# Smaller token lists for the large experts: 11 and 7 blocks in place of 12 and 8, with mixed blocks of four equal tiles

## The chip, the cores and the metric

The kernel runs on one core of a Trainium2 chip. The metric is the time of one execution in device microseconds (us); the time before is the median of three runs. Bytes are counted in thousands and millions here; a "piece" of weights is 1.05 MB.

## What is computed

Two layers of a diffusion backbone over 256 latent and 256 context tokens of width 1024. Layer 0 mixes by grouped attention and a Fourier branch, layer 1 by differential attention; after each stands a mixture of 16 experts, of which every token takes two:

```
tok = h.reshape(-1, shape[-1])
g_idx = argmax(tok @ w_group + b_group)
e_sel = (tok @ w_router + b_router) of that group
top_p, top_i = lax.top_k(softmax(e_sel), 2)
for each expert:  y = (silu(tok @ wg) * (tok @ wu)) @ wd
                  acc += gate[:, None] * y
```

Each expert's three matrices are 1024 by 512, 1024 by 512 and 512 by 1024, in float32. Layer 0 sends 512 tokens through the mixture, layer 1 only the 256 latent ones.

## The kernel before, in words

**Lists and blocks.** The kernel does not run all tokens through all experts. It sorts the experts of a layer by their token counts (rank 0 has most; two experts in layer 0 and four in layer 1 are left out of the sorting and stand at the last ranks) and gives rank r a list of `CAPS[layer][r]` places (line 32). `PLAN` (line 37) packs the lists into blocks of 128 places, which `block_plan` (line 55) turns into lists of tiles (first place, width, rank): `("m", r)` is one list of 128, `("p", r, s)` two tiles of 64, `("q", ...)` four tiles of 32, and `("w", 0, 1)` cuts the two lists of 192 into two whole blocks and one block of two tiles of 64. That makes 12 blocks in layer 0 and 8 in layer 1. Tokens beyond a list's places go to a slow overflow pass at the layer's end, which runs only if a list overflows (line 1752).

**Products.** A block b has three products: G (gate), U (up) and D (down), 8 chunks of 512 columns each, 24 in all. In layer 0 `products` (line 73) orders them G U of block b, then D of block b-1; in layer 1 the order is written out in `TURNS` (line 69). `gate_up` and `down` (lines 1645 and 1673) issue them. A block of one list in layer 0 is `solo`: the weights are split into a high and a low part by ScalarE and VectorE (line 317, 318) and each chunk is three matmuls with full rows (lines 321 to 323). Every other block multiplies float32 directly (lines 1658 and 1691): each tile of the block is one matmul per chunk into its own stripe of output partitions, and the trace has two rows for each such matmul.

**Lists in layer 0.** `fetch_rows` (line 1265) makes the row numbers of a block: for each of 4 groups of tokens and both choices of expert VectorE compares places with numbers (`hot`, line 1399, output `oh`), and TensorE multiplies (line 1275, output `tok`); then the rows are gathered by an indirect DMA. D writes its result to the scratch tensor `yd` by DMAs on ScalarE's queue (line 1709), two for each tile. In layer 1 rows are picked by matmuls (line 1326, `pick`) and spread back by matmuls (line 1596, `sp`).

**Weights.** Each of an expert's three matrices is two pieces `we`. A piece is loaded once into a room; there are 16 rooms in layer 0 and 18 in layer 1, and a load waits until the room's last piece has been read. The loads stand in one queue on SP (line 216) in the order in which the products first use them (`Experts`, line 993). For ranks that are sorted SP must first read the rank's expert from `perm` (line 1020), which the routing makes. The loads of SP and the writes of `yd` use the same eight completion semaphores in turn, so that a load whose turn falls on the semaphore of a write waits for that write to land. Which instruction stands where on TensorE, VectorE and ScalarE is set by a scheduler when the kernel is built.

Of the kernel before, what the change touches and what calls it, by code (L numbers as in the profile page):

```python
# [11 lines left out]
F32 = mybir.dt.float32  # L12
F32R = mybir.dt.float32r
BF16 = mybir.dt.bfloat16
I32 = mybir.dt.int32
AF = mybir.ActivationFunctionType
ALU = mybir.AluOpType
AX = mybir.AxisListType

P = 128  # L20
# [9 lines left out]


CAPS = (
    (192, 192) + (128,) * 4 + (64,) * 10,
    (192, 192) + (128,) * 2 + (32,) * 12,
)

PLAN = (
    (("p", 14, 15), ("m", 2), ("p", 12, 13), ("m", 3), ("p", 10, 11), ("w", 0, 1), ("m", 4), ("m", 5), ("p", 8, 9),
     ("p", 6, 7)),
    (("q", 12, 13, 14, 15), ("m", 3), ("m", 2), ("w", 0, 1), ("q", 8, 9, 10, 11), ("q", 4, 5, 6, 7)),  # L40
)
MAXSLOTS = max(sum(c) for c in CAPS)

# [1 line left out]
def bases(layer):  # L45

    out, n = [0] * NE, 0
    for _, *rs in PLAN[layer]:
        for r in rs:
            out[r] = n  # L50
            n += CAPS[layer][r]
    return out


def block_plan(layer):

    base, blocks = bases(layer), []
    for kind, *rs in PLAN[layer]:
        if kind == "w":
            pair = [(base[r] + 128, 64, r) for r in rs]  # L60
            ones = [[(base[r], 128, r)] for r in rs]
            blocks += [pair] + ones if layer else [ones[0], pair, ones[1]]
        else:
            blocks.append([(base[r], 128 // len(rs), r) for r in rs])
    return blocks

TURNS = ("G0 U0 G1 U1 D0 D1 G6 G4 U6 U4 G3 G5 D6 U3 D4 U5 D3 D5 G7 G2 U2 U7 D2 D7")


def products(layer):
# [3 lines left out]
    if layer:  # L76
        return [("GUD".index(t[0]), int(t[1:])) for t in TURNS.split()]
    out, n = [], len(block_plan(layer))
# [87 lines left out]
def hybrid_kernel(ctx: ExitStack, tc: tile.TileContext, A: dict, dbg=None):  # L166
    nc = tc.nc
    V, S, T, G = nc.vector, nc.scalar, nc.tensor, nc.gpsimd
# [25 lines left out]
    def right(name):  # L194
        return Open(name, "right")
# [26 lines left out]
    def mm(name="mm"):  # L222
        return psum.tile([P, 512], F32, name=name, tag="mm", bufs=5)
# [4 lines left out]
    def aux(name):  # L228
        return psum.tile([P, 512], F32, name=name, tag="aux", bufs=1)
# [25 lines left out]
    def C(name):  # L255
        a, b = CC.at[name]
        return cst[:, a:b]
# [16 lines left out]
    ones = pool.tile([P, P], BF16, name="ones")  # L274
    V.memset(ones, 1.0)
    tokid = pool.tile([P, 4, 2], BF16, name="tokid")
# [766 lines left out]
    def moe(l, ntb, experts, yp, yT, finish, w_o, place, after_loads):  # L1043
# [151 lines left out]
        def tl(shape, name, dt=F32):  # L1195
            return rt.tile([P] + shape, dt, name=name)
# [63 lines left out]
        blocks = block_plan(l)  # L1260
# [3 lines left out]
        un = right("units")  # L1264
# [3 lines left out]
        def fetch_rows(i, hot):  # L1268

            ps = aux("tok")  # L1270
            for tb in range(ntb):
                for k in range(2):
                    o = un.tile([P, P], BF16, name="oh", bufs=2)
                    hot(o, tb, k)
                    T.matmul(ps[:, 0:2], o, tokid[:, tb, :], start=(tb == 0 and k == 0),
                             stop=(tb == ntb - 1 and k == 1))
            ix = un.tile([P, 1], I32, name="ix", bufs=8)
            with nc.allow_low_precision("whole numbers below 512"):
                V.reduce_sum(ix, ps[:, 0:2], axis=AX.X)
            xg[i] = un.tile([P, D], F32, name="xg", bufs=2)  # L1280
            G.indirect_dma_start(out=xg[i], out_offset=None, in_=h2d[0:NT, :],
                                 in_offset=bass.IndirectOffsetOnAxis(ap=ix[:, 0:1], axis=0))
# [92 lines left out]
        slot, gate, ridx = [], [], []  # L1375
# [3 lines left out]
        slots = tl([2, ntb], "slots")  # L1379
        V.reduce_sum(slots, tmp, axis=AX.X)  # L1380
        slot = [slots[:, i, :] for i in range(2)]


        def runs(i):

            out = []
            for s0, n_, _ in blocks[i]:
                if out and sum(out[-1]) == s0:
                    out[-1] = out[-1][0], out[-1][1] + n_
                else:  # L1390
                    out.append((s0, n_))
            return out

        def fetch(i):

            def hot(o, tb, k):
                c = 0
                for s0, n_ in runs(i):
                    V.tensor_scalar(o[:, c:c + n_], C("iota128")[:, 0:n_], float(s0), slot[k][:, tb:tb + 1],
                                    op0=ALU.add, op1=ALU.is_equal)  # L1400
                    c += n_

            fetch_rows(i, hot)
# [50 lines left out]
        hots, rel = {}, {}  # L1454
# [85 lines left out]
        def combine(tb):  # L1540

            ya = got.pop(tb)
            S.activation(ya[0], ya[0], AF.Copy, scale=early[0][:, tb, :])
            V.scalar_tensor_tensor(ya[1], ya[1], early[1][:, tb, :], ya[0], op0=ALU.mult, op1=ALU.add)
            V.tensor_tensor(out=ya[1], in0=ya[1], in1=g2[:, tb // 2, :], op=ALU.mult)
            V.tensor_tensor(out=xt[:, tb, :], in0=xt[:, tb, :], in1=ya[1], op=ALU.add)
# [65 lines left out]
        def a_turn(bi, q):  # L1612
            if q == 0:
                aTs[bi] = [un.tile([P, 4, P], F32R if solo[bi] else F32, name="aT", bufs=AB)
                           for _ in range(1 + solo[bi])]
            pt = tr()
            for f in range(2):
                c = 256 * q + 128 * f
                T.transpose(pt[:, 128 * f:128 * f + 128], sgs[bi][:, c:c + 128], ident)
            a = [t[:, 2 * q:2 * q + 2, :] for t in aTs[bi]]  # L1620
            src = pt[:, 0:256].rearrange("p (k t) -> p k t", k=2)
            if solo[bi]:
                split(*a, src)
            else:
                V.tensor_copy(a[0], src)
            if q:
                sgs.pop(bi)
# [11 lines left out]
        def split_to(i, k):  # L1639
            for c in chunks[len(parts):]:  # L1640
                if c[0] > i + 1 or KT * (c[0] - i) + c[1] > k + WB - 1:
                    break
                parts[c] = [un.tile([P, 512], F32R, name=name, bufs=WB) for name in ("wh", "wl")]
                split(*parts[c], weights_at(*c))
# [27 lines left out]
        def down(bi, amid, final):  # L1672
            late = bi not in aTs
            if late:
                a_turn(bi, 0)
            if final:
                a_turn(bi, 1)
                combine(2)
            ps = [mm("dn") for h in range(2)]
            for f in range(4):  # L1680
                if f == 1 and late and not final:
                    a_turn(bi, 1)
                amid(f)
                for h in range(2):
                    split_to(now[0], 2 * f + h)
                    if solo[bi]:
                        mm3(ps[h], [t[:, f, :] for t in aTs[bi]], parts[now[0], 2 * f + h], f == 0, f == 3)
                        continue
                    c = 0
                    for _, n_, r in blocks[bi]:  # L1690
                        T.matmul(ps[h][c:c + n_], aTs[bi][0][:, f, c:c + n_],  # L1691
                                 part(experts.w[r, 2], f)[:, 512 * h:512 * h + 512], start=(f == 0), stop=(f == 3))
                        c += n_
            spread_some(4)
            if l:
                if bi == [b for which, b in ops if which == 0][-1]:

                    S.activation(lam[:, 6:7], aTs[bi][0][:, 0, 0:1], AF.Sqrt, bias=eps, scale=0.0)
                ship(bi, ps)
            elif final:  # L1700
                finish_ctx(ps)
            else:
                c = 0
                y = [un.tile([P, 512], F32, name="y", bufs=1 if l else YB) for h in range(2)]
                V.tensor_copy(y[0], ps[0])
                S.copy(y[1], ps[1])
                for s0, n_, _ in blocks[bi]:
                    for h in range(2):
                        sent = S.dma_start(yd[s0:s0 + n_, 512 * h:512 * h + 512], y[h][c:c + n_, :])
                    c += n_  # L1710
                if bi == len(blocks) - 2:
                    for _ in range(6):
                        experts.issue(1, queue=S)
# [38 lines left out]
        with tc.If(rv > 0):  # L1752
# [16 lines left out]
            with tc.For_i(0, NE, 1) as e:  # L1769
# [3 lines left out]
                with tc.If(nc.values_load(some[0:1, 0:1], min_val=0, max_val=1) > 0):  # L1773
                    ws = []
                    for i in range(3):
                        ws.append([])
                        for h in range(2):
                            w, src = weights(pick, i, h)
# [4 lines left out]
                    for tb in range(ntb):  # L1783
# [4 lines left out]
                        for half in range(2):  # L1788
                            pt = tr()
                            for j in range(4):  # L1790
                                kt = 4 * half + j
                                c = slice(128 * kt, 128 * kt + 128)
                                if l == 0:
                                    T.transpose(pt[:, 128 * j:128 * j + 128], xr[:, c], ident)
                                for n in range(len(exact)):
                                    T.matmul(pt[:, 128 * j:128 * j + 128], exact[n][tb][:, c], identb, start=(n == 0),
                                             stop=(n == len(exact) - 1))
                            S.copy(xT_[:, 4 * half:4 * half + 4, :], pt.rearrange("p (k t) -> p k t", k=4))
                        gu = []
                        for which in range(2):  # L1800
                            ps = tr("gu")
# [11 lines left out]
                        for h in range(2):  # L1813
                            ps = tr("dn")
                            for f in range(4):
# [3 lines left out]
                                                   op0=ALU.mult, op1=ALU.mult)  # L1819
# [7 lines left out]
        if l:  # L1827
            for tb, h in itertools.product(tbs, range(2)):
                c = slice(512 * h, 512 * h + 512)
# [132 lines left out]
```

## Time and profile before

| | |
|---|---|
| median of 3 runs (lowest to highest) | 1064.69 us (1059.69 to 1064.75) |
| the profiled execution | 1066.53 us, of it 1064.7 us span |
| TensorE (PE) busy | 985.5 us, 93% |
| VectorE (DVE) busy | 556.2 us, 52% |
| ScalarE (ACT) busy | 397.3 us, 37% |
| bytes moved by DMA | 309.85 MB, 291 GB/s on average |
| mean granted TensorE clock | 0.976 |

The span is the time from the first to the last instruction; 1.8 us of the execution lie outside it. Busy time of TensorE overlaps waits in part, since ends of matmuls are modelled, so lengths of stretches are read from starts of instructions in the timeline. Products of layer 0's experts run from 274 to 568 us of the span, those of layer 1's from 825 to 1050 us.

### The profile page before, as it was taken

What the parts mean: (1) busy time and instruction counts of PE and PEld (TensorE: products, weight loads), DVE (VectorE), ACT (ScalarE), POOL (GpSimd) and SP (SyncE); (2) the same over time, 40 slices, a digit from 0 to 9 for tenths busy, and PEclk for the clock granted to TensorE, in tenths of its full rate; (3) what the DMA queues carried; (4) which work ended last, traced back from release to release, by engine and by line L of the source; (5) the groups of instructions that cost most, each with busy time, mean ns of one, the idle gap of its engine ahead of it and who ended that gap; (6) DMA issues with size and microseconds to landing.
All of it is one profiled execution on the core that took longest, in us unless ns stands there. A gap on an engine that the chain in (4) does not pass through costs nothing. (4 is left out here: it accounts for less than half of the span.)

```text
span 1064.7 us, 14592 instructions
## 1 busy us (share of the span) xinstructions
PE 985.5 (93%) x5205; PEld 574.6 (54%) x5205; DVE 556.2 (52%) x1354; ACT 397.3 (37%) x817; POOL 49.2 (5%) x73
## 2 busy tenths in 40 slices
PE   4899999897999989999986999998878999999995
PEld 3666555686555435566422668885556444434532
DVE  3564465767565545578325745627877422214324
ACT  4254343643234324567204525327873311100211
POOL 3000100100000000000021000000000000000000
PEclk9999999999999999999989999999998999999998
DMA  9988877536779998989896593333164999999991
GB/s 284 367 332 323 342 312 275 201 136 212 289 312 411 358 422 307 367 332 357 333 383 228 215 398 128 119 119 158 41 220 139 383 420 419 420 374 408 380 374 41
DMA packets 66950, 309.85 MB, mean 291 GB/s; under 512 B 6544, under 2 KB 14944, under 8 KB 37176
## 3 DMA queue, kind: packets, MB, share of 16 engines
q1 hardware_dynamic: 56408, 277.01, 67.0%
q0 software_dynamic: 5984, 19.26, 5.3%
q10 hardware_dynamic: 4480, 12.59, 3.3%
q8 instruction: 43, 0.70, 0.3%
q14 instruction: 35, 0.29, 0.1%
HBM read 299.85 MB, written 8.98 MB: 290 GB/s over the span
## 5 line engine op out<-in xcount | busy, mean ns | idle before, releaser
L1658 PE MATMUL gu<-we,xT 128*64 128x512 f32 (+1 forms) x512 | 119.6, 616 | 3.2 <-DMA we<-in_w_up_dram 3.2
L1691 PE MATMUL dn<-we,aT 128*64 128x512 f32 (+2 forms) x480 | 119.1, 606 | 2.8 <-DMA we<-in_w_down_dram 2.6
L317 ACT CAST wh<-we 128x512 fp32r<-128x512 f32 x144 | 85.5, 621 | 64.1 <-PE dn L322 24.3
L1658 PE MATMUL gu<-we,xt 128*32 128x512 f32 (+2 forms) x448 | 105.2, 596 | 0.0
L318 DVE TENSOR_TENSOR wl<-we,wh 128x512 fp32r<-128x512 f32 x144 | 92.2, 687 | 20.9 <-ACT wh L317 19.2
L321 PE MATMUL mm<-wh,hT 128*128 128x512 f32 x248 | 101.5, 409 | 1.8 <-ACT hT L317 1.8
L322 PE MATMUL mm<-wh,hT 128*128 128x512 f32 x248 | 97.8, 394 | 0.7 <-DVE hT L318 0.7
L323 PE MATMUL mm<-wl,hT 128*128 128x512 f32 x248 | 98.1, 395 | 0.0
L1691 PEld LDWEIGHTS dn<-we,aT 128*64 128x64 f32 (+2 forms) x480 | 36.0, 134 | 66.1 <-issue 59.1
L1658 PEld LDWEIGHTS gu<-we,xT 128*64 128x64 f32 (+1 forms) x512 | 33.7, 133 | 62.3 <-issue 54.6
L1658 PEld LDWEIGHTS gu<-we,xt 128*32 128x32 f32 (+2 forms) x448 | 36.3, 136 | 57.2 <-issue 55.1
L318 DVE TENSOR_TENSOR wl<-wi,wh 128x512 fp32r<-128x512 f32 x52 | 35.7, 690 | 48.3 <-ACT wh L317 34.6
L1669 DVE TENSOR_TENSOR sg<-sg,gu 128x256 f32<-128x256 f32 x40 | 15.2, 417 | 83.8 <-PE gu L1658 80.8
L321 PEld LDWEIGHTS mm<-wh,hT 128*128 128x128 f32 x248 | 46.9, 189 | 20.5 <-issue 8.4
L317 ACT CAST wh<-wi 128x512 fp32r<-128x512 f32 x52 | 32.1, 621 | 64.0 <-PE mm L322 59.6
L323 PEld LDWEIGHTS mm<-wl,hT 128*128 128x128 f32 x248 | 46.9, 189 | 12.2 <-issue 0.8
L322 PEld LDWEIGHTS mm<-wh,hT 128*128 128x128 f32 x248 | 47.0, 189 | 10.6 <-DVE hT L318 1.0
L317 ACT CAST y<-y 128x512 fp32r<-128x512 f32 x16 | 9.9, 618 | 97.6 <-DVE y L1589 85.1
L321 PE MATMUL mm<-wo,yT 128*128 128x512 f32 x96 | 40.9, 426 | 2.3 <-ACT wo L317 2.3
L350 PE MATMUL ada<-wada,cs 128*32 128x512 f32 x320 | 40.8, 600 | 0.5 <-DMA wada<-in_w_ada_dram 0.5
L1664 ACT ACTIVATE sg<-gu 128x512 f32<-128x512 f32 x20 | 11.9, 597 | 77.7 <-PE gu L1658 72.0
L323 PE MATMUL mm<-lo,yT 128*128 128x512 f32 x96 | 39.2, 410 | 1.1 <-DVE lo L318 1.0
(367 smaller groups left out, 1658.0 us busy)
## 6 DMA issues: line engine op xcount, KB each, us to landing
we<-in_w_gate_dram SPq DMA_DIRECT2D x64, 1024.0 KB, 10.3
we<-in_w_up_dram SPq DMA_DIRECT2D x62, 1024.0 KB, 8.7
we<-in_w_down_dram SPq DMA_DIRECT2D x60, 1024.0 KB, 15.9
wada<-in_w_ada_dram SPq DMA_DIRECT2D x48, 1024.0 KB, 8.9
wi<-in_w_in_odd_dram SPq DMA_DIRECT2D x12, 1024.0 KB, 8.9
win<-in_w_in_even_dram SPq DMA_DIRECT2D x4, 1024.0 KB, 11.7
wo<-in_w_out_even_dram SPq DMA_DIRECT2D x4, 1024.0 KB, 8.3
we<-in_w_down_dram ACTq DMA_DIRECT2D x4, 1024.0 KB, 14.7
```

The lines of the kernel that those rows point to most:

```text
L317: S.copy(hi, src)
L318: V.tensor_tensor(out=lo, in0=src, in1=hi.bitcast(F32), op=ALU.subtract)
L321: T.matmul(ps, a[0], b[0], start=start, stop=False)
L322: T.matmul(ps, a[1], b[0], start=False, stop=False)
L323: T.matmul(ps, a[0], b[1], start=False, stop=stop)
L350: T.matmul(ps[32 * j:32 * j + 32], cs[:, kt, :], part(w, k)[:, 512 * j:512 * j + 512], start=(kt == 0), stop=(kt == KT - 1))
L1658: T.matmul(ps[c:c + n_], xTs[bi][0][:, kt, c:c + n_], part(experts.w[r, which], kt), start=(kt == 0), stop=(kt == KT - 1))
L1664: S.activation(parted(sgs[bi], 4), by_part(ps, 4), AF.Silu)
L1669: V.tensor_tensor(out=sg[:, c], in0=sg[:, c], in1=up[:, c], op=ALU.mult)
L1691: T.matmul(ps[h][c:c + n_], aTs[bi][0][:, f, c:c + n_], part(experts.w[r, 2], f)[:, 512 * h:512 * h + 512], start=(f == 0), stop=(f == 3))
```

## The change

`CAPS` and `PLAN` are new. In layer 0 ranks 0 and 1 get 160 places in place of 192, ranks 2 and 3 get 96 in place of 128. A new kind `("x", ...)` keeps the first 128 places of ranks 0 and 1 as whole blocks, and packs what is left into mixed blocks of four tiles of 32: 32 places of rank 0 and 96 (three tiles) of rank 2 in one, the same of ranks 1 and 3 in another. Layer 0 has 11 blocks: 4 solo, 5 of two tiles, 2 mixed. In layer 1 ranks 0 and 1 get 160, rank 3 gets 64, and one mixed block holds 32 places of rank 0, 32 of rank 1 and 64 of rank 3; layer 1 has 7 blocks: 3 whole, 3 of four lists, 1 mixed. `TURNS` is written anew for 7 blocks. In `fetch_rows` one matmul serves both choices of a token: VectorE writes the comparison for the first choice and adds that for the second. D writes one `yd` DMA for each run of places that follow each other, no longer one for each tile.

```diff
 CAPS = (
-    (192, 192) + (128,) * 4 + (64,) * 10,
-    (192, 192) + (128,) * 2 + (32,) * 12,
+    (160, 160) + (96,) * 2 + (128,) * 2 + (64,) * 10,
+    (160, 160) + (128, 64) + (32,) * 12,
 )
 PLAN = (
-    (("p", 14, 15), ("m", 2), ("p", 12, 13), ("m", 3), ("p", 10, 11), ("w", 0, 1), ("m", 4), ("m", 5), ("p", 8, 9),
-     ("p", 6, 7)),
-    (("q", 12, 13, 14, 15), ("m", 3), ("m", 2), ("w", 0, 1), ("q", 8, 9, 10, 11), ("q", 4, 5, 6, 7)),
+    (("p", 14, 15), ("m", 4), ("p", 12, 13), ("p", 10, 11), ("x", 0, 1, 2, 3), ("m", 5), ("p", 8, 9), ("p", 6, 7)),
+    (("q", 12, 13, 14, 15), ("m", 2), ("x", 0, 1, 3), ("q", 8, 9, 10, 11), ("q", 4, 5, 6, 7)),
 )
+        elif kind == "x":
+            ones = [[(base[r], 128, r)] for r in rs[:2]]
+            tiles = lambda *rs: [(base[r] + n, 32, r) for r in rs for n in range(128 if CAPS[layer][r] > 128 else 0,
+                                                                                CAPS[layer][r], 32)]
+            blocks += ones + [tiles(*rs)] if len(rs) == 3 else [ones[0], tiles(rs[0], rs[2]), ones[1],
+                                                                tiles(rs[1], rs[3])]
-TURNS = ("G0 U0 G1 U1 D0 D1 G6 G4 U6 U4 G3 G5 D6 U3 D4 U5 D3 D5 G7 G2 U2 U7 D2 D7")
+TURNS = ("G0 U0 D0 G2 U2 G4 U4 D2 G3 U3 D4 D3 G6 U6 G1 G5 U1 D6 U5 D1 D5")
...
             for tb in range(ntb):
-                for k in range(2):
-                    o = un.tile([P, P], BF16, name="oh", bufs=2)
-                    hot(o, tb, k)
-                    T.matmul(ps[:, 0:2], o, tokid[:, tb, :], start=(tb == 0 and k == 0),
-                             stop=(tb == ntb - 1 and k == 1))
+                o = un.tile([P, P], BF16, name="oh", bufs=2)
+                hot(o, tb)
+                T.matmul(ps[:, 0:2], o, tokid[:, tb, :], start=(tb == 0), stop=(tb == ntb - 1))
...
-                    V.tensor_scalar(o[:, c:c + n_], C("iota128")[:, 0:n_], float(s0), slot[k][:, tb:tb + 1],
-                                    op0=ALU.add, op1=ALU.is_equal)
+                    if tb == 0:
+                        rel[s0] = un.tile([P, 2, ntb], F32, name="rel", bufs=4)
+                        V.tensor_scalar(rel[s0], slots, -float(s0), None, op0=ALU.add)
+                    at = [rel[s0][:, k, tb:tb + 1] for k in range(2)]
+                    V.tensor_scalar(o[:, c:c + n_], C("iota128")[:, 0:n_], at[0], None, op0=ALU.is_equal)
+                    V.scalar_tensor_tensor(o[:, c:c + n_], C("iota128")[:, 0:n_], at[1], o[:, c:c + n_],
+                                           op0=ALU.is_equal, op1=ALU.add)
...
-                for s0, n_, _ in blocks[bi]:
+                for s0, n_ in runs(bi):
                     for h in range(2):
                         sent = S.dma_start(yd[s0:s0 + n_, 512 * h:512 * h + 512], y[h][c:c + n_, :])
```

The order of instructions, at two places. First TensorE in layer 0, where the direct products of the block behind the whole block of rank 0 begin (`gu` is the output of G and U, `dn` of D, `xT` and `aT` the inputs, `we` a piece of weights, `wh` and `wl` a split one). Before:

```order
L322 MATMUL gu<-wh,xT 128x512
L323 MATMUL gu<-wl,xT 128x512
L1691 MATMUL dn<-we,aT 64x512 x2
L1619 MATMUL tr<-cst,sg 128x128 x4
L1658 MATMUL gu<-we,xT 64x512
L1691 MATMUL dn<-we,aT 64x512 x6
L1658 MATMUL gu<-we,xT 64x512
```

Of the change:

```order
L328 MATMUL gu<-wh,xT 128x512
L329 MATMUL gu<-wl,xT 128x512
L1700 MATMUL dn<-we,aT 64x512 x2
L1628 MATMUL tr<-cst,sg 128x128 x4
L1667 MATMUL gu<-we,xT 32x512
L1700 MATMUL dn<-we,aT 64x512 x6
L1667 MATMUL gu<-we,xT 32x512
```

Both stretches end the split products of rank 0's whole block and begin the next block; what moved is that this block's matmuls are four tiles of 32 columns a chunk (`32x512`) and no longer two of 64.

Second SP's queue in layer 1, from the last load before the routing is needed. Before:

```order
L216 DMA we<-in_w_up_dram 128x2048 x8
L1020 TENSOR_LOAD perm
L1020 ISA x2
L216 ISA
L216 DMA we<-in_w_gate_dram 128x2048
```

Of the change:

```order
L222 DMA we<-in_w_up_dram 128x2048 x8
L222 DMA we<-in_w_down_dram 128x2048 x2
L1026 TENSOR_LOAD perm
L1026 ISA x2
L1026 TENSOR_LOAD perm
```

Before, the first load behind the 16 of G and U of block 0 is the gate of a sorted rank, which needs `perm`; now two loads of D of block 0 stand ahead of `perm`, ten reads of `perm` follow each other, and the other six loads of that D stand behind them.

## Rows read from the trace of the kernel before

**Rows 1.** The page's 40 slices: share of the DMA engines and rate.

```profile
DMA  9988877536779998989896593333164999999991
GB/s 284 367 332 323 342 312 275 201 136 212 289 312 411 358 422 307 367 332 357 333 383 228 215 398 128 119 119 158 41 220 139 383 420 419 420 374 408 380 374 41
```

**Rows 2.** TensorE's groups by shape: names, shapes, count | busy us, mean ns.

```profile
L1658 PE MATMUL gu<-we,xT 128*64 128x512 f32 x384 | 104.2, 623 | 3.2 <-DMA we<-in_w_up_dram 3.2
...
L321 PE MATMUL gu<-wh,xT 128*128 128x512 f32 x96 | 39.1, 408 | 0.8 <-ACT wh L317 0.8
```

**Rows 3.** TensorE's timeline, layer 0, a block of two tiles: start, length, count.

```profile
318.81 7.04 PE L1658 MATMUL gu<-we,xT 128*64 128x512 f32 x32
325.78 0.20 PE L1275 MATMUL tok<-tokid,oh 128*128 128x2 bf16 x2
...
330.44 4.50 PE L1658 MATMUL gu<-we,xT 128*64 128x512 f32 x18
...
336.36 1.04 PE L1451 MATMUL tr<-cst,xg 128*128 128x128 f32 x8
```

**Rows 4.** The same timeline, a split block, from one chunk's first matmul to the next's.

```profile
299.73 0.40 PE L321 MATMUL gu<-wh,xT 128*128 128x512 f32 x1
...
300.42 0.40 PE L321 MATMUL gu<-wh,xT 128*128 128x512 f32 x1
```

**Rows 5.** The same timeline: first and last product of layer 0.

```profile
274.17 1.07 PE L1658 MATMUL gu<-we,xT 128*64 128x512 f32 x2
...
562.62 5.34 PE L1691 MATMUL dn<-we,aT 128*64 128x512 f32 x14 [2.63 <-DMA we<-in_w_down_dram]
```

**Rows 6.** Lists in layer 0: TensorE's timeline, then VectorE's group.

```profile
386.04 0.37 PE L1275 MATMUL tok<-tokid,oh 128*128 128x2 bf16 x2 [0.19 <-DVE oh L1399]
386.60 0.37 PE L1275 MATMUL tok<-tokid,oh 128*128 128x2 bf16 x2 [0.18 <-DVE oh L1399]
...
L1399 DVE TENSOR_SCALAR oh<-cst,slots 128x128 bf16<-128x128 f32 x80 | 20.1, 283 | 28.6 <-PE tok L1275 27.4
```

**Rows 7.** SP's waits, 268 to 545 us: total us, times, longest.

```profile
SPq L216 <- DMA yd<-y: 117.8, 11, 16.9
```

**Rows 8.** TensorE's timeline in layer 1's products.

```profile
824.76 7.07 PE L1658 MATMUL gu<-we,xT 128*32 128x512 f32 x64
...
835.19 2.85 PE L1326 MATMUL pick<-pick,h 128*128 128x128 bf16 x48
...
847.42 10.47 PE L1658 MATMUL gu<-we,xt 128*128 128x512 f32 x24
...
979.42 0.66 PE L1619 MATMUL tr<-cst,sg 128*128 128x128 f32 x4
...
993.14 2.43 PE L1596 MATMUL sp<-y,hot 128*128 128x512 f32 x8
...
1042.55 7.08 PE L1691 MATMUL dn<-we,aT 128*32 128x512 f32 x56
```

**Rows 9.** SP's timeline in layer 1: start, length and count of loads.

```profile
825.11 1.78 SPq L216 DMA_DIRECT2D we<-in_w_gate_dram  x2
...
847.95 22.78 SPq L216 DMA_DIRECT2D we<-in_w_gate_dram  x10
872.85 22.74 SPq L216 DMA_DIRECT2D we<-in_w_up_dram  x10
...
927.64 7.80 SPq L216 DMA_DIRECT2D we<-in_w_down_dram  x4
953.79 10.11 SPq L216 DMA_DIRECT2D we<-in_w_gate_dram  x10
...
1003.41 18.43 SPq L216 DMA_DIRECT2D we<-in_w_down_dram  x10
```

**Rows 10.** SP's waits, 820 to 1064 us: total us, times, longest.

```profile
SPq L216 <- PE gu L1658: 46.9, 15, 16.2
```

**Rows 11.** The page's DMA issues: a piece that finds the engines idle.

```profile
wo<-in_w_out_odd_dram SPq DMA_DIRECT2D x4, 1024.0 KB, 5.0
```

More of the change, by code (lines that the diff above doesn't have):

```diff
@@ L1394, in fetch, with hot @@
         def fetch(i):
-            def hot(o, tb, k):
+            def hot(o, tb):
                 c = 0
                 for s0, n_ in runs(i):
-                    V.tensor_scalar(o[:, c:c + n_], C("iota128")[:, 0:n_], float(s0), slot[k][:, tb:tb + 1],
-                                    op0=ALU.add, op1=ALU.is_equal)
+                    if tb == 0:
[5 more added lines that the diff above has]
+                                           op0=ALU.is_equal, op1=ALU.add)
                     c += n_
```

## The prediction

> **What bounds the kernel now.** I read the slices of the page first, then TensorE's groups and timeline in the two stretches that the change touches, then SP's timeline and waits there. The slices show two different stretches [rows 1]. In layer 0 (slices 11 to 22) the rate moves between 228 and 422 GB/s and the DMA share between 6 and 9: the engines have room. In layer 1 (slices 32 to 39) it is never under 374 and stands at 419 or 420 in three slices running: there the weights come about as fast as this trace ever shows.
>
> Layer 0's products run from 274.2 to 568.0 us, 293.8 us [rows 5]. Their chunks have two prices. A chunk of two tiles is four rows, and 32 rows take 7.04 us: 0.88 us [rows 3]. A split chunk is three matmuls, and from one to the next it is 300.42 - 299.73 = 0.69 us [rows 4]. The groups give the counts: 384 rows of G and U in two tiles are 96 chunks, six blocks of 16; 96 split ones are six blocks as well [rows 2]. With 24 chunks to a block, 6 x 24 x 0.88 + 6 x 24 x 0.69 = 226.1 us of the 293.8 are products. The rest is transposes, lists and waits. SP waits there 117.8 us for writes of yd to land, 11 times [rows 7]: its loads run behind the blocks' results, so they come in step with the work and not at the engines' rate.
>
> Layer 1's products run from 824.8 to 1049.6 us, 224.9 us [rows 8]. All its chunks cost the same: four tiles, eight rows, 7.07 us for 64 rows, 0.884 us; a whole block, two rows, 10.47 / 12 = 0.873 us [rows 8]. SP stands behind the routing until 825.1, then issues a piece every (872.85 - 847.95) / 10 = 2.49 us [rows 9], which at 1.05 MB is the 421 GB/s of the slices. Between about 935 and 953.8 it issues nothing [rows 9], and its longest wait for TensorE to free a room is 16.2 us [rows 10]: rooms held by unread pieces, not the engines, made that hole. The last pieces are issued by 1021.8 [rows 9], and TensorE is still busy with earlier work when they land. So work and weights are nearly level here, and whichever is left longer after the change sets the end.
>
> **The change in layer 0.** Before 6 split blocks and 6 of two tiles, after 4 split, 5 of two tiles and 2 of four tiles. I give the mixed chunk the 0.88 us of the paired one; layer 0 has none, and the nearest row is layer 1's 0.884 [rows 8]. After: 4 x 24 x 0.69 + 7 x 24 x 0.88 = 66.2 + 147.8 = 214.1, **12.0 us less**. The two split blocks that go take few microseconds with them, since split chunks are the cheap ones for TensorE; the block that goes is worth its difference only.
>
> The block less also takes 8 transposes of its input, 1.04 us [rows 3], and 4 of its activation, 0.66 [rows 8]: **1.7 us**. The casts and subtractions of 48 split chunks go too, but they ran beside TensorE; I count nothing. If they had not been covered, the gain would be larger.
>
> Lists: 11 fetched blocks with 8 matmuls each are 88, now 10 with 4 are 40; 48 go. Their price has two ends. Where they stand singly between direct chunks they are dear: from 325.78 to 334.94 us there are 8 chunks (7.04) and 8 of them, 2.1 us, 0.26 each [rows 3]. Where several lists are made in a row, VectorE's comparisons set the pace: two matmuls each 0.56 us, released by `oh` [rows 6], which is two comparisons at 283 ns; the comparisons remain 96 (80 and, for the two blocks with two runs, 16 more), so there nothing is gained. The added form, which compares and adds, has no row of this shape; I give it the same 283 ns. From 48 x 0.26 = 12.7 to 0, I take 0.12 each, **5.8 us**, nearer to the lower end as a third of the lists stand in such a row.
>
> The fewer yd writes (32 to 20) are off TensorE's path: I count them at nothing, since what SP waits for is the result that they carry. What remains of the 293.8 us, some 38 with waits for weights, I leave as it is, because the loads come in step with the blocks. Layer 0: 12.0 + 1.7 + 5.8 = **19.5 us less**, between 13.7 and 26.4.
>
> **The change in layer 1.** TensorE loses a whole block: 24 x 0.884 = 21.2 us, one pick 2.85, one spread 2.43, four transposes 0.66 [rows 8]: 27.1. The mixed block takes the place of the paired one at the same price. Work alone would then need 224.9 - 27.1 = 197.8 us. The weights don't get fewer: 80 pieces were issued behind the routing, now 78, since D of block 0 comes third and two of its pieces fit into rooms that are free ahead of the routing. Of the ten reads of `perm` that now follow each other no row shows the price; between 0 and the 0.57 us that SP needs from one issue to the next they are up to 6 us, but the first rooms come free only at 824.8 + 3.5 = 828.3, when half of G of block 0 is done, so I start the stream at 829. A lone piece lands 5.0 us after its issue [rows 11], the 77 behind it each 2.49 later: 829 + 5.0 + 191.7 = 1025.7. The last D then has four chunks left, 3.5 us: 1029.2 in place of 1049.6, 20.4 less. That is the weights' bound, and longer than the work's.
>
> It holds if SP never waits for a room. The mixed block makes that unlikely: pieces of rank 0 and 1 are read by two products each and held in between, and D4 and D3 bring only four new pieces before G6 and U6 need sixteen. I charge half of the longest wait seen, 8 us [rows 10]: **12.4 us less**. Ends: 20.4 without such a wait, 4.4 with a whole one of 16 us. What is late next is D6, U5 and D5, whose pieces TensorE will wait for.
>
> One rule speaks against the new tiles. The rows show no loss from cutting a chunk in four: 0.884 us against 0.873 for a whole block [rows 8]. The Trainium skill (TensorE: Matmul & The Clock Gate, "Why this matters for your kernels") says that three tiles of 32 columns side by side are 2.38 times as fast as one after the other, not three times. By that figure a chunk of four would cost about 1.11 us by estimate, and layer 0 would gain 11 us less; the trace disagrees. So the sum goes by the rows.
>
> **Sum.** 19.5 + 12.4 = 31.9 us. The profiled execution took 1066.5 us (span 1064.7), so 1034.6; the median of the runs lies 1.8 below it, so **1033**. A measurement of this kernel can tell some 0.5%, 5.3 us, from no change.
>
> **Rivals.**
> - *More than the sum.* The lists stand mostly between chunks and give 12.7, and layer 1 follows the weights without a hole: 26.4 + 20.4 = 46.8, 1018. For it: the run of lists is only a part of layer 0. Against: 15 waits of SP for G and U chunks in layer 1 [rows 10].
> - *Rooms eat layer 1.* The lists give nothing and a whole hole of 16 us returns: 13.7 + 4.4 = 18.1, 1047.
> - *The mixed tiles are dear*: tiles that don't run side by side as well as those of four experts, because one expert's weights pass three times. The dearest direct chunks in the rows are those broken into by lists, 9.16 / 8 = 1.14 us [rows 3]; at that price layer 0 loses 48 x 0.26 = 12.5 us, layer 1 hides its share behind the weights: 1045. Against it: 0.884 [rows 8]. This is the way in which the rule cited above would come out.
> - *No change.* Layer 0's loads do not follow the faster blocks, layer 1's neither: TensorE waits for what it no longer computes, about 1062. Against: layer 0 leaves the DMA engines room [rows 1], its loads wait for results [rows 7].
> - *Slower: the lists are too short.* From one expert with more tokens than places on, the overflow pass runs. In layer 0 it costs per expert at least its six pieces, 5.0 + 5 x 2.49 = 17.5 us, and four groups of tokens of 24 chunks, 4 x 21: over 100 us, 1134 or more. The trace has no counts; routing the reference's own inputs gives, sorted, 142, 142, 89, 81, 77, 69, 55 in layer 0 (places 160, 160, 96, 96, 128, 128, 64) and 141, 127, 70, 56, 27 in layer 1 (160, 160, 128, 64, 32). All fit, the tightest by 5 to 8 places; rounding on the chip would have to move that many tokens.
>
> **How the numbers follow.** Forecast 0.60; more than the sum 0.15; rooms eat layer 1 0.13; dear tiles 0.04; no change 0.04; lists too short 0.04. Faster by over 0.5% are the first four, 0.92; within 0.5% 0.04; slower 0.04. The range goes from the first rival's 1018 to the second's 1047, which leaves the last two cases out.
>
> **What would show it.** Right: products of layer 0 over about 274 us; mixed rows (128*32) in layer 0 with 64 rows in some 7.1 us; 40 tok matmuls; layer 1's products over about 212 us, its DMA share at 9 or more nearly throughout, and TensorE waiting for pieces of U5, D6 and D5 near the end. Wrong in a step: 64 mixed rows in 9 us (tiles dear), a stretch of layer 0 as long as before with longer waits for `we` (weights), a hole of 10 us or more in SP's issues in layer 1 (rooms), any instruction of the overflow pass (lists). If layer 0 gains over 30 us, its waits were not kept, and the lists or the writes of yd had cost more than I counted.

## Result and profile of the changed kernel

The changed kernel takes **1035.87 us** (median of 4 runs, 1034.03 to 1036.96) against 1064.72 us in the same comparison: ratio **0.9741, 95% interval 0.9718 to 0.9764**, 28.85 us less. The forecast was 1033, between 1018 and 1047. Its profiled execution took 1034.03 us (span 1032.2), 1.8 below the median, while that of before lay 1.8 above its own; so the two traces differ by 32.5 us, 3.7 more than the medians.

| stretch (from TensorE's timeline) | before | changed | difference | forecast |
|---|---|---|---|---|
| layer 0, first product to last | 293.8 | 281.3 | -12.5 | -19.5 |
| between the layers' products | 256.8 | 253.1 | -3.7 | 0 |
| layer 1, first product to last | 224.9 | 208.4 | -16.5 | -12.4 |

So the total came out, but by two errors of opposite sign: layer 0 gained 7.0 us less than forecast, layer 1 4.1 more. The 3.7 us between the layers are no effect of the change (last section). The page's slices of the changed kernel (DMA share and rate) show layer 1 fuller than before [rows 1]: from the 33rd slice on, seven in a row stand at 405 to 421 GB/s.

```profile
DMA  9988888463798998978997695425056799999993
GB/s 281 365 307 314 340 338 289 155 225 138 290 395 351 420 372 349 402 307 311 391 399 262 253 347 184 156 90 204 1 176 215 279 419 419 421 405 421 418 420 140
```

TensorE's timeline of the changed kernel (start, length, count): first and last product of layer 0, mixed chunks in G and D, first and last product of layer 1.

```profile
273.76 1.07 PE L1667 MATMUL gu<-we,xT 128*64 128x512 f32 x2
...
442.94 13.92 PE L1667 MATMUL gu<-we,xT 128*32 128x512 f32 x128
...
480.07 3.64 PE L1700 MATMUL dn<-we,aT 128*32 128x512 f32 x32
...
547.61 7.42 PE L1700 MATMUL dn<-we,aT 128*64 128x512 f32 x32
...
808.12 7.07 PE L1667 MATMUL gu<-we,xT 128*32 128x512 f32 x64
...
1012.86 3.62 PE L1700 MATMUL dn<-we,aT 128*32 128x512 f32 x20 [0.59 <-DMA we<-in_w_down_dram]
```

The last products end at 555.0 and 1016.5. A mixed chunk is eight rows, and 128 rows take 13.92 us: 0.87 us each, as the 0.88 of two tiles [rows 3]. The three tiles that share one expert's weights cost nothing extra. The Trainium skill (TensorE: Matmul & The Clock Gate, "Why this matters for your kernels") gives a gain of 2.38 for three 32-column tiles side by side, from which the prediction estimated 1.11 us a chunk; the measured 0.87 us disagrees, and decides here. No run has such a tile by itself.

Where layer 0 lost is its last block, p(6,7). Its G and U begin at 512.9, and TensorE waits for pieces again and again:

```profile
515.79 3.65 PE L1667 MATMUL gu<-we,xT 128*64 128x512 f32 x14 [1.18 <-DMA we<-in_w_gate_dram]
520.85 1.04 PE L1667 MATMUL gu<-we,xT 128*64 128x512 f32 x2 [1.42 <-DMA we<-in_w_gate_dram]
524.83 3.68 PE L1667 MATMUL gu<-we,xT 128*64 128x512 f32 x6 [2.94 <-DMA we<-in_w_gate_dram]
...
537.29 8.78 PE L1667 MATMUL gu<-we,xT 128*64 128x512 f32 x30 [2.35 <-DMA we<-in_w_up_dram]
```

The marked waits add up to 7.9 us, but they cost more. The windows view (length; busy us and count by engine; granted clock; DMA share; GB/s) has a granted clock of 0.66 over the 15 us from 520, and 0.50, the lower of TensorE's two levels (1.2 and 2.4 GHz), right behind the longest wait; at 541, the waits being over, it is back at 0.99:

```profile
520.00:535.00 15.00, 10.81 (x22) 2.86 (x22) 0.64 (x2) 1.18 (x2) 5.67 (x6) 0.66 1.02 425
...
525.00:530.00 5.00, 4.66 (x10) 1.27 (x10) 0.64 (x2) 0.00 (x0) 3.78 (x5) 0.50 1.01 425
...
541.00:547.00 6.00, 5.42 (x24) 1.62 (x20) 0.75 (x2) 0.00 (x0) 0.00 (x0) 0.99 1.02 419
```

So the clock falls behind waits for a DMA. The Trainium skill (TensorE: Matmul & The Clock Gate, "HAM oscillation — how this bites in real kernels") describes matmuls that run throttled after each such wait; the trace agrees in kind, with waits of 1.2 to 2.9 us where the page's example has 3 to 5. From its first G to its last D this block took 37.8 us before (530.21 to 567.96) and 42.1 now (512.94 to 555.03). The rest of layer 0 went from 256.0 to 239.2 us, 16.8 less.

SP's timeline tells when these pieces were sent for: the four of gate from 502.18 to 516.5, while TensorE wanted the first at 512.9.

```profile
502.18 14.32 SPq L222 DMA_DIRECT2D we<-in_w_gate_dram  x4
```

And its waits tell for what it stood (us, times, longest): as before [rows 7], for writes of yd. The first line is from 240 to 560 us, the second from 485 to 516, when these pieces were due:

```profile
SPq L222 <- DMA yd<-y: 108.4, 11, 18.1
...
SPq L222 <- DMA yd<-y: 23.8, 3, 11.4
```

Not all loads stand in SP's queue, though. The last six of layer 0, two pieces of up and four of down for the last block, are issued by ScalarE behind the last of its writes (line 1722; line 1713 in the kernel before). In the changed kernel TensorE waits for none of these six; the four waits above are for pieces that SP sent.

Layer 1 is the opposite. The windows view of its products:

```profile
812.00:818.00 6.00, 5.88 (x53) 1.65 (x49) 5.66 (x36) 4.55 (x6) 0.00 (x0) 1.00 0.60 210
818.00:824.00 6.00, 5.75 (x54) 1.54 (x46) 0.33 (x4) 0.00 (x0) 0.00 (x0) 1.00 1.01 425
...
830.00:860.00 30.00, 30.00 (x202) 13.94 (x202) 10.29 (x32) 4.14 (x8) 0.00 (x0) 1.00 1.01 418
860.00:900.00 40.00, 40.00 (x233) 17.65 (x226) 9.01 (x21) 3.88 (x7) 0.00 (x0) 1.00 1.01 420
900.00:925.00 25.00, 25.00 (x190) 11.33 (x189) 11.59 (x23) 4.52 (x8) 0.00 (x0) 1.00 1.00 405
...
960.00:1005.00 45.00, 39.75 (x179) 13.59 (x177) 11.85 (x21) 4.05 (x6) 0.00 (x0) 0.92 1.01 420
```

From 818 us to 1005 the weights flow at 405 to 425 GB/s without a hole. Yet SP waited for rooms about as long as before [rows 10] (waits from 800 us on):

```profile
SPq L222 <- PE gu L1667: 43.6, 13, 11.2
```

The pieces that were issued already kept the engines busy all that time: in this stretch a piece lands 18 to 20 us after its issue (medians of gate, up and down), and the longest wait is 11.2. The trace of before shows the same. SP issued nothing there from 935.4 to 953.8 us [rows 9], yet the engines' share over these 18.4 us was 0.96; they ran dry only at their end:

```profile
935.00:945.00 10.00, 10.00 (x52) 3.30 (x50) 0.00 (x0) 0.60 (x1) 0.00 (x0) 1.00 1.01 416
945.00:955.00 10.00, 9.36 (x49) 2.81 (x49) 2.88 (x4) 1.23 (x2) 0.00 (x0) 1.00 0.83 333
```

TensorE waits near the end, for up pieces of U5 (three times, 3.4 us) and a down piece of D5 (0.6): two of the three that the prediction named. Behind the waits for U5, of at most 1.4 us each, the granted clock is 0.50 from 985 to 990 us. Some 3 us are lost to the weights' bound by the time that the last piece lands: the DMA engines take up the loads behind the routing at 814, 5.9 us after the layer's first product (4.2 in the prediction), and are done with the weights at about 1012, 204 us after it (201).

### The profile page after: what moved, and what is told of

The parts are those of the page before. It is cut to its first block, busy times and chain, and to the rows that moved or that the text cites. A ratio compares the mean times of both kernels' runs of the same rounds, so it can differ in the third digit from the quotient of the medians.

```text
span 1032.2 us, 14454 instructions
## 1 busy us (share of the span) xinstructions
PE 948.2 (92%) x5271; PEld 537.8 (52%) x5271; DVE 515.7 (50%) x1288; ACT 363.3 (35%) x755; POOL 46.9 (5%) x72
## 5 line engine op out<-in xcount | busy, mean ns | idle before, releaser
L1667 PE MATMUL gu<-we,xT 128*32 128x512 f32 (+1 forms) x704 | 132.1, 611 | 7.9 <-DMA we<-in_w_gate_dram 5.5
L1700 PE MATMUL dn<-we,aT 128*32 128x512 f32 (+2 forms) x592 | 121.5, 598 | 0.9 <-DMA we<-in_w_down_dram 0.6
L1667 PE MATMUL gu<-we,xt 128*32 128x512 f32 (+1 forms) x480 | 96.9, 614 | 3.4 <-DMA we<-in_w_up_dram 3.4
L1667 PEld LDWEIGHTS gu<-we,xT 128*32 128x32 f32 (+1 forms) x704 | 36.5, 125 | 80.7 <-issue 69.8
L323 ACT CAST wh<-we 128x512 fp32r<-128x512 f32 x96 | 56.6, 620 | 48.7 <-PE dn L328 15.3
L324 DVE TENSOR_TENSOR wl<-we,wh 128x512 fp32r<-128x512 f32 x96 | 62.2, 686 | 21.8 <-ACT wh L323 18.7
L1700 PEld LDWEIGHTS dn<-we,aT 128*32 128x32 f32 (+2 forms) x592 | 36.3, 123 | 65.1 <-issue 59.0
L1667 PEld LDWEIGHTS gu<-we,xt 128*32 128x32 f32 (+1 forms) x480 | 31.5, 128 | 55.6 <-issue 46.1
L327 PE MATMUL mm<-wo,yT 128*128 128x512 f32 x96 | 39.6, 412 | 2.4 <-ACT wo L323 2.4
L328 PE MATMUL mm<-wo,yT 128*128 128x512 f32 x96 | 37.5, 392 | 0.0
## 6 DMA issues: line engine op xcount, KB each, us to landing
yd<-y ACTq DMA_DIRECT2D x16, 256.0 KB, 7.8
```

The lines of the kernel that those rows point to most:

```text
L323: S.copy(hi, src)
L324: V.tensor_tensor(out=lo, in0=src, in1=hi.bitcast(F32), op=ALU.subtract)
L327: T.matmul(ps, a[0], b[0], start=start, stop=False)
L328: T.matmul(ps, a[1], b[0], start=False, stop=False)
L1667: T.matmul(ps[c:c + n_], xTs[bi][0][:, kt, c:c + n_], part(experts.w[r, which], kt), start=(kt == 0), stop=(kt == KT - 1))
L1700: T.matmul(ps[h][c:c + n_], aTs[bi][0][:, f, c:c + n_], part(experts.w[r, 2], f)[:, 512 * h:512 * h + 512], start=(f == 0), stop=(f == 3))
```

## The experiments

All were timed in five rounds. "Ratio" is to the kernel before, timed on the same chip, with its 95% interval. Microseconds are differences of medians; by the ratios they come out within 2 us of these, and a difference between two changed kernels is known to some 4 us.

**The four parts alone.** Each puts one part of the diff into the kernel before.

*Layer 0's blocks alone* (old lists, old writes, old layer 1):

```diff
-    (192, 192) + (128,) * 4 + (64,) * 10,
+    (160, 160) + (96,) * 2 + (128,) * 2 + (64,) * 10,
...
+    (("p", 14, 15), ("m", 4), ("p", 12, 13), ("p", 10, 11), ("x", 0, 1, 2, 3), ("m", 5), ("p", 8, 9), ("p", 6, 7)),
```

> The kernel before with the new lists sizes and blocks of layer 0 alone (lists, writes of yd and layer 1 as before). Theory A, the prediction's sum: 12.0 us for cheaper chunks and 1.7 for the block less, waits as before: 13.7 us less, 1051 us against 1064.7 (ratio 0.987), products of layer 0 over 280 us in place of 293.8. Theory B, what the two traces suggest: the last block waits longer for its weights and gives back some 6 us, so 7 to 8 us less, 1057 us (ratio 0.993), products over 286 us, and G and U of the last block stretched over more than 30 us where TensorE's own rows for them are 14.

Measured: 1057.18 us, ratio 0.9944 (0.9923 to 0.9966), 7.2 us less; products of layer 0 over 288.3 us. That is theory B's time; the products became 5.5 us shorter, a little less than it says. The last block shows where the rest went:

```profile
518.52 3.65 PE L1664 MATMUL gu<-we,xT 128*64 128x512 f32 x14 [1.35 <-DMA we<-in_w_gate_dram]
522.52 1.04 PE L1664 MATMUL gu<-we,xT 128*64 128x512 f32 x2 [0.35 <-DMA we<-in_w_gate_dram]
525.19 1.93 PE L1664 MATMUL gu<-we,xT 128*64 128x512 f32 x6 [1.63 <-DMA we<-in_w_gate_dram]
...
533.69 8.78 PE L1664 MATMUL gu<-we,xT 128*64 128x512 f32 x30 [2.49 <-DMA we<-in_w_up_dram]
...
551.98 6.67 PE L1697 MATMUL dn<-we,aT 128*64 128x512 f32 x14 [2.64 <-DMA we<-in_w_down_dram]
```

It runs 42.5 us (516.13 to 558.65), 4.8 more than before. This kernel has more writes of yd than the changed one, 40 against 24 (32 before), since every tile of 32 still has its own two.

*The lists alone:*

```diff
-                for k in range(2):
-                    o = un.tile([P, P], BF16, name="oh", bufs=2)
-                    hot(o, tb, k)
-                    T.matmul(ps[:, 0:2], o, tokid[:, tb, :], start=(tb == 0 and k == 0),
-                             stop=(tb == ntb - 1 and k == 1))
+                o = un.tile([P, P], BF16, name="oh", bufs=2)
+                hot(o, tb)
+                T.matmul(ps[:, 0:2], o, tokid[:, tb, :], start=(tb == 0), stop=(tb == ntb - 1))
```

> The kernel before with one matmul for both choices of a token alone: 88 list matmuls become 44. Theory A, the prediction's price of 0.12 us each: 44 x 0.12 = 5.3 us less, 1059.4 us (ratio 0.995). Rival: VectorE's comparisons set the pace and nothing is gained, 1064.7 (ratio 1.000). Rival: the end of layer 0 is set by its weights, and what the lists give up is waited for at the last block: 0 to 2 us less, with the saved time standing as longer waits of the last G and U.

Measured: 1058.1 us, ratio 0.9936 (0.9913 to 0.996), 6.3 us less for 44 matmuls, 0.14 each. The price of 0.12 stands; neither rival does. The size is not sharp: the interval is 4 to 9 us, and in the one trace the products are 9.0 us shorter (284.8), 2.2 of them in the last block. In the changed kernel VectorE's compare-and-add takes 346 ns where I gave it 283 (line, operation, count, busy us, mean ns; idle time before):

```profile
L1408 DVE SCALAR_TENSOR_TENSOR oh<-cst,rel,oh 128x128 bf16<-128x128 f32 x32 | 10.3, 346 | 0.2
```

*Layer 1 alone* (its line of `CAPS`, of `PLAN`, and `TURNS`):

```diff
-    (192, 192) + (128,) * 2 + (32,) * 12,
+    (160, 160) + (128, 64) + (32,) * 12,
...
+TURNS = ("G0 U0 D0 G2 U2 G4 U4 D2 G3 U3 D4 D3 G6 U6 G1 G5 U1 D6 U5 D1 D5")
```

> The kernel before with layer 1's new lists, blocks and order alone (layer 0, lists and writes as before). Theory A, the prediction: weights' bound 20.4 us less, 8 us given back to waits for rooms: 12.4 us less, 1052.3 us (ratio 0.988). Theory B, after the trace of the change: the weights' stream runs almost without a hole, 16 to 20 us less, 1045 to 1049 us (ratio 0.981 to 0.985), products of layer 1 over 205 to 209 us. The stretch between the layers (256.8 us before, 253.1 in the change) stays at 257 if the 3.7 us there have nothing to do with layer 1, and falls to about 253 if they belong to layer 1's new order of loads.

Measured: 1048.82 us, ratio 0.9853 (0.9828 to 0.9879), 15.6 us less; products over 208.7 us, and the weights' stream has no hole:

```profile
834.00:1020.00 186.00, 179.97 (x1177) 76.72 (x1170) 49.08 (x118) 21.35 (x38) 0.00 (x0) 0.99 1.01 418
```

That is nearer to theory B than to A. The stretch between the layers is 259.4 us: the 3.7 us there don't belong to layer 1.

*The writes of yd alone:*

```diff
-                for s0, n_, _ in blocks[bi]:
+                for s0, n_ in runs(bi):
```

> The kernel before with one write of yd for each run of places alone (fewer writes, nothing else). Theory A, the prediction: nothing, 1064.7 us (ratio 1.000, within 0.002). Rival: since loads take turns with the writes on eight completion semaphores, fewer writes mean fewer loads that stand behind one: SP's 117.8 us of waits for yd fall by a third and layer 0 gains 2 to 5 us, 1060 to 1063 us.

Measured: 1063.5 us, ratio 0.9989 (0.9972 to 1.0005): nothing that can be told from no change, as forecast. SP's waits for yd in line 223 stay at 116.1 us, 10 times: 24 writes in place of 32, but a load still stands behind one.

The four parts give 7.2 + 6.3 + 15.6 + 0.9 = 30.0 us; together they gave 28.85. The parts add up, each known to some 2 us.

**Does the order of layer 1 matter?**

```diff
-TURNS = ("G0 U0 D0 G2 U2 G4 U4 D2 G3 U3 D4 D3 G6 U6 G1 G5 U1 D6 U5 D1 D5")
+TURNS = ("G0 U0 D0 G5 G2 U5 U2 G4 G3 D5 U4 D2 U3 D4 D3 G6 G1 U1 U6 D1 D6")
```

> The changed kernel with layer 1's products in the order of the kernel before, carried over to seven blocks (G0 U0 D0 G5 G2 U5 U2 G4 G3 D5 U4 D2 U3 D4 D3 G6 G1 U1 U6 D1 D6). Theory A, the prediction's fear: in such an order pieces stay in their rooms unread and the stream of weights has a hole, here of 8 to 16 us more than in the changed kernel, 1044 to 1052 us against 1035.9 (ratio to the kernel before 0.981 to 0.988). Theory B: a wait for a room costs nothing while pieces already issued are still landing, and the order hardly matters: within 3 us of the changed kernel, 1033 to 1039 us (ratio 0.970 to 0.976).

Measured: 1041.69 us, ratio 0.978 (0.9748 to 0.9812): in the median 5.8 us over the changed kernel, between the two theories, and the intervals overlap (0.9718 to 0.9764). The trace gives layer 1's products 210.9 us, 2.5 more, and the stretch between the layers, where nothing differs, 5.7 more. The waits of SP in this kernel (from 810 us):

```profile
SPq L222 <- PE gu L1667: 9.5, 9, 6.3
...
SPq L222 <- PE dn L1700: 8.5, 2, 8.3
```

SP waits for rooms 18 us here and 57 us in the changed kernel (43.6 for G and U, 13.7 for D), and the kernel with less of it is not the faster one. The order is worth a few microseconds at most; how many is not settled. But no hole as feared opens: the DMA share is 1.01 or 1.02 from 830 to 1000 us.

**What holds the last block's weights?** Two attempts on the changed kernel: the writes of yd from another queue, and another order of the last three blocks.

```diff
-                        sent = S.dma_start(yd[s0:s0 + n_, 512 * h:512 * h + 512], y[h][c:c + n_, :])
+                        sent = G.dma_start(yd[s0:s0 + n_, 512 * h:512 * h + 512], y[h][c:c + n_, :])
```

> The changed kernel with the writes of yd issued by GpSimd and no longer by ScalarE, so that no load of weights shares a completion semaphore with one. Theory A: the loads of layer 0 are held back by the writes' landings (108 us of SP's waits), and without them the last block's weights come earlier: its G and U shrink from 33 us towards 14, 8 to 15 us less than the changed kernel, 1021 to 1028 us (ratio to the kernel before 0.959 to 0.966). Theory B: the rooms and the rate of the weights hold the loads just as long, and the writes only name the wait: within 3 us of 1035.9 (ratio 0.970 to 0.976). Rival: GpSimd stands behind the writes and fetches the rows of the blocks late: 3 us or more slower than the changed kernel.

Measured: **1023.49 us, ratio 0.9611 (0.9582 to 0.9641)**, 12.4 us less than the changed kernel and faster than both kernels of this study. SP's waits from 240 to 560 us have no yd any more, and wait for rooms instead:

```profile
SPq L222 <- PE gu L1667: 57.1, 18, 19.6
...
SPq L222 <- PE dn L1700: 43.0, 6, 17.9
```

The gate of the last block is sent for from 483.16 on, 19 us sooner, and TensorE's timeline has one wait left in that block, for a piece of D:

```profile
483.16 6.99 SPq L222 DMA_DIRECT2D we<-in_w_gate_dram  x4
```

```profile
518.83 8.80 PE L1667 MATMUL gu<-we,xT 128*64 128x512 f32 x40
528.26 0.83 PE L1628 MATMUL tr<-cst,sg 128*128 128x128 f32 x4 [0.62 <-DVE sg L1678]
529.21 4.50 PE L1700 MATMUL dn<-we,aT 128*64 128x512 f32 x18
535.78 3.65 PE L1700 MATMUL dn<-we,aT 128*64 128x512 f32 x14 [2.06 <-DMA we<-in_w_down_dram]
```

The granted clock in these 15 us is 1.00 in place of 0.66:

```profile
519.00:534.00 15.00, 13.97 (x62) 4.35 (x60) 1.57 (x4) 2.27 (x3) 5.73 (x6) 1.00 1.02 422
```

Layer 0's products take 265.9 us, 15.4 less; the last block alone 28.9 (510.57 to 539.43), 13.2 less. Theory A holds. The Trainium skill (Trainium Kernel Development and Optimization, "Key Constraints") says that issuing DMAs from several engines at once only saves issue time. The measurement goes beyond that, and decides: the 24 issues took ScalarE 0.33 us each, 7.9 us over the whole layer, and moving them was worth 12.4, because of what stands behind them. Nor does TensorE gain much from a freer ScalarE: its waits for split weights in layer 0 fall from 2.0 to 1.2 us, those for pieces from 7.9 to 2.1. But ScalarE's own six loads go out sooner too (up at 512.71 for 516.87, down from 513.81 for 523.15), and this was not tried apart from SP's.

```diff
-... ("x", 0, 1, 2, 3), ("m", 5), ("p", 8, 9), ("p", 6, 7)),
+... ("x", 0, 1, 2, 3), ("p", 8, 9), ("m", 5), ("p", 6, 7)),
```

> The changed kernel with layer 0's last three blocks in the order p(8,9), m 5, p(6,7) in place of m 5, p(8,9), p(6,7). Theory A: the last block is late because two blocks of twelve pieces each stand at the end; with a block of six pieces between them its weights are further ahead, its waits of some 19 us shrink by 4 to 10 us, 1026 to 1032 us (ratio to the kernel before 0.964 to 0.969). Theory B: the sum of the weights over the layer sets the end, whatever their order: within 2 us of 1035.9 (ratio 0.971 to 0.975).

Measured: 1039.83 us, ratio 0.9762 (0.9734 to 0.9791). No gain: theory A falls. Waits moved from the pieces of the last block (7.9 us, now 4.5) to the splits of block m 5 (2.0 us, now 5.5): TensorE's waits from 270 us on now read

```profile
PE dn L1700 <- DMA we<-in_w_down_dram: 4.1, 3, 2.6
PE gu L327 <- ACT wh L323: 3.5, 3, 2.0
...
PE dn L327 <- ACT wh L323: 2.0, 1, 2.0
```

**Do the writes explain the missing 6 us of the new blocks?** The same edit in the kernel before, without and with layer 0's new blocks.

> The kernel before with the writes of yd issued by GpSimd alone: what the loads' turn behind the writes costs in the old blocks. Theory A: the kernel before pays for it as the changed one does (117.8 us of SP's waits against 108.4), 10 to 15 us less, 1049 to 1055 us (ratio 0.986 to 0.991). Theory B: before, TensorE had more work of its own to lie beside the loads, and the cost grew with the change: 2 to 7 us less, 1057 to 1062 us (ratio 0.993 to 0.998).

Measured: 1054.83 us, ratio 0.99 (0.9876 to 0.9924), 9.7 us less, just under theory A's 10 and above B's 7. The kernel before had the loss too, in the same place: its last block now runs 25.2 us (530.85 to 556.02) in place of 37.8, which is the whole shortening of layer 0 (281.3 us against 293.8), without a wait for a piece:

```profile
530.85 5.37 PE L1658 MATMUL gu<-we,xT 128*64 128x512 f32 x24
...
537.51 8.80 PE L1658 MATMUL gu<-we,xT 128*64 128x512 f32 x40
...
547.89 8.13 PE L1691 MATMUL dn<-we,aT 128*64 128x512 f32 x32
```

Which loads were late differs, however. In the kernel before, the three waits of the last block (two here, the third in [rows 5]) are all for the six pieces that ScalarE sends; none is for a piece of SP's, for all of SP's 117.8 us behind yd. TensorE's timeline and ScalarE's queue before:

```profile
544.30 1.07 PE L1658 MATMUL gu<-we,xT 128*64 128x512 f32 x2 [1.03 <-DMA we<-in_w_up_dram]
547.54 6.35 PE L1658 MATMUL gu<-we,xT 128*64 128x512 f32 x14 [2.16 <-DMA we<-in_w_up_dram]
...
536.94 2.32 ACTq L216 DMA_DIRECT2D we<-in_w_up_dram  x2
539.78 2.37 ACTq L216 DMA_DIRECT2D we<-in_w_down_dram  x4
```

With the writes on GpSimd:

```profile
531.33 0.93 ACTq L216 DMA_DIRECT2D we<-in_w_up_dram  x2
532.43 2.57 ACTq L216 DMA_DIRECT2D we<-in_w_down_dram  x4
```

From the block's first G on, that is 6.7 and 9.6 us before, 0.5 and 1.6 now. SP's gate pieces also went out sooner (from 502.06 in place of 512.02); what that adds was not tried apart.

> The kernel before with layer 0's new blocks and the writes of yd issued by GpSimd (lists with two matmuls and layer 1 as before); to be read against the run of the kernel before with its writes on GpSimd. Theory B: without the writes ahead of the loads the blocks give their whole 13.7 us: products of layer 0 13 to 15 us shorter than there, against the 5.5 to 7 us that the same blocks gave with the writes on ScalarE. Theory A: the missing 6 us were lost to something else (rooms, the rate of the weights, the split chunks), and the blocks give 5 to 8 us here as well.

Measured: 1042.43 us, ratio 0.979 (0.9766 to 0.9814). Against the run just above, the blocks give 12.4 us, their products 281.3 - 269.5 = 11.8 us, where they gave 7.2 and 5.5 with the writes on ScalarE. So theory B holds but for some 2 us of the 13.7; the last block still waits once, for 2.2 us:

```profile
538.04 3.65 PE L1697 MATMUL dn<-we,aT 128*64 128x512 f32 x14 [2.20 <-DMA we<-in_w_down_dram]
```

**Both attempts together:** the writes on GpSimd and m 5 between the two pairs.

> The changed kernel with the writes of yd issued by GpSimd and the last three blocks of layer 0 in the order p(8,9), m 5, p(6,7). Theory A: with the loads free of the writes, the block of six pieces between the two of twelve lets the last weights come in time: 3 to 5 us less than with the writes on GpSimd alone (1023.5), 1018 to 1021 us (ratio 0.956 to 0.959). Theory B: TensorE waits for only 2 us of pieces there, so there is nothing to win and the order's cost of some 3 us stays: 1023 to 1027 us (ratio 0.961 to 0.965).

Measured: 1029.36 us, ratio 0.9657 (0.9626 to 0.9688), with runs from 1024.8 to 1033.3: slower in the median by 5.9 us than with the writes alone, though the intervals overlap; layer 0's products take 273.9 us in its trace, 265.9 there. Theory A falls, and the median lies over theory B's 1023 to 1027 as well; the other order is no improvement in either kernel.

## Why the prediction was right, and where it was not

- **The blocks' work, 12.0 + 1.7 us: right in size.** Free of the writes they gave 12.4 us (11.8 in the products). Mixed tiles at the price of paired ones: right, 0.87 us.
- **"What remains of the 293.8 us, some 38 with waits for weights, I leave as it is, because the loads come in step with the blocks": wrong, by about 6 us.** The loads do come in step, but with the writes of yd, and at the end of layer 0 two blocks of twelve pieces each follow each other. It is the prediction's own sign "a stretch of layer 0 as long as before with longer waits for `we`": 42.1 us for 37.8. Work that is taken out ahead of them does not make these pieces land sooner by as much. Of 16.8 us gained in the rest of layer 0 the last block took 4.3 back. The runs with and without the writes on ScalarE show it: 5.5 against 11.8 us for the same blocks (with 40 writes, so the 6 us are not exactly those of the change).
- **Lists, 5.8 us: right within the interval.** 6.3 us (4 to 9) measured alone, for 44 of the 48 matmuls.
- **Writes of yd at nothing: right for their number** (0.9 us, within the interval), though 24 are left and not 20, as a mixed block has two runs of places. But the reason given, that SP waits for the result and not for the write, was half of it: the queue that carries them is worth 9.7 us in the kernel before.
- **Layer 1, "I charge half of the longest wait seen, 8 us": wrong.** The products became 16.5 us shorter, so about 4 of the 20.4 were lost, not 8, and not in a hole: 1.00 to 1.02 of the DMA share from 818 to 1005 us. "Rooms held by unread pieces, not the engines, made that hole" misread the trace of before: SP paused for 18 us there, the DMA engines hardly (0.96). The longest wait for a room is no measure of a hole, since issued pieces go on landing while SP waits. Some 3 of the 4 us are a later start and a slightly lower rate of the stream (204 for 201 us until the last piece). The weights' bound, 20.4, was the better estimate, and U5 and D5 waited for their pieces as said.
- **The sum: right by cancellation, and so partly by luck.** 19.5 + 12.4 = 31.9 forecast; 12.5 + 16.5 = 29.0 in the traces' two layers, 28.85 in the medians.
- **The rivals.** "Dear tiles", "lists too short" and "no change" fall. "More than the sum" was right that layer 1 has no hole (16.5 us of its 20.4), and "rooms eat layer 1" in neither of its terms. A case in which the last block of layer 0 gives time back was missing.

## What to carry to other kernels

Before a saving ahead of a stretch that is fed by DMA is counted in full, ask which load the last block of the stretch waits for, and what that load stood behind: here writes of results, on its own queue (before) or on another with which it shared completion semaphores (after). Moving the writes was worth 9.7 us and 12.4. A queue's wait for room costs only where the engines run dry meanwhile, so read the DMA share of that stretch and not the length of the wait. And two terms that are off by 7 and 4 us in opposite directions look like a good forecast: compare stretch by stretch.

## What was not expected of the hardware

The stretch between the two layers has the same code in the changed kernel and in the kernel with m 5 late, yet took 253.1 and 259.0 us. The windows view of its last part, up to layer 1's first product, has a granted clock of 1.00 in the first and of 0.89 in the second:

```profile
767.00:808.10 41.10, 33.06 (x196) 25.63 (x195) 34.15 (x93) 20.91 (x36) 1.11 (x2) 1.00 0.72 250
```

```profile
768.60:815.60 47.00, 39.56 (x203) 30.04 (x202) 36.19 (x97) 23.49 (x40) 1.11 (x2) 0.89 0.69 241
```

TensorE waits there for the router's small steps, and its clock fell behind them in one execution and not in the other. The whole difference, 47.0 against 41.1 us, lies in this part, where TensorE's nearly equal number of instructions was busy 39.6 us and 33.1. What decides it is open. The odd one is the changed kernel's: in all eleven other traces the last 41 us of this stretch have a granted clock of 0.88, and the whole of it takes 256.8 us (before) to 261.1. So the 3.7 us by which it is shorter in the table belong to that one execution, and they are as much as the two traces differ beyond the medians.
